# A 90-degree rotation of an 8192 x 8192 matrix: VectorE's grid copies move one output later in its order

## The chip, the cores and the metric

The kernel runs on one core of one Trainium2 chip. The metric is device time in microseconds (us) for one execution. The comparison value is the median of several runs.

## The reference

```python
def setup_inputs():
    return {"x": np.random.randn(8192, 8192).astype(np.float32), "k": 1}

def reference(x, k):
    return np.rot90(x, k)
```

With k = 1, output element (i, j) is x[j, 8191 - i]: a transpose and a reversal of the columns. Nothing is computed. 268.44 MB are read and 268.44 MB are written.

## The kernel before, in words

**Macros, tiles, outputs.** The matrix is cut into 16 macros (`macros`, line 54), numbered kk, each 1024 rows by 4096 columns. A macro arrives as T = 8 row tiles of 128 rows by 4096 columns (2 MB each) and leaves as J = 8 outputs (2 MB each). An output takes one chunk of 512 columns from all eight row tiles and is written as 512 rows by 1024 columns of the result. So 128 loads and 128 stores of 2 MB are made in all. Loads are numbered m = 8 kk + t and outputs n = 8 kk + j. In what follows, a dash marks the next macro: tile 0' is tile 0 of macro kk + 1.

**The grid.** A macro is held in a grid of 8 x 8 slots of 512 columns (`grid` in SBUF, line 61). Five corner slots are in PSUM (`corner`, line 62), and four of the grid places so freed serve as staging buffers for TensorE (`STAGES`, line 24). In an even macro a tile fills a row of slots and an output reads a column. In an odd macro it is the other way round. So the slots that output j has been read out of are just those that tile j of the next macro needs, and one grid holds two macros that interleave.

**Buffers.** There are five SBUF buffers of 2 MB. Loads use three at first and, after the ninth load, only two (`load_buf`, line 80). Outputs rotate over three (`out_buf`, line 83), except the last eight, which use all five.

**What each engine does.**

- SyncE (line 132) issues the loads. A load waits until the load that last used its buffer has been copied to the grid (`s_copy`, line 137).
- VectorE (line 146) does two things. `place(m)` (line 149) waits for the landing of tile m and copies its 4096 columns from the buffer to its grid slots, in one or two instructions (line 156). This frees the load buffer. `to_stage` (line 159) copies 512 columns per partition, reversed, to a staging buffer (line 166). A call waits until TensorE is done with the stage it reuses (line 163).
- TensorE (line 212) transposes each staged half block by four 128 x 128 matmuls with the identity into one of three PSUM banks (line 221).
- ScalarE (line 237) copies each bank to the output buffer (line 258), eight copies of 512 columns to an output, and then issues the store (line 265). Before an output's first copy it waits for the store that last used the buffer (line 244).

**VectorE's order.** It is written out by hand in lines 188 to 209, and it sets when the loads' buffers come free and when outputs start. An output with j > 0 is eight `to_stage` calls. Output 0 of a macro is made in `first(kk)` (line 173): eight `to_stage` calls, one for each tile. The first seven read from the grid. The eighth reads tile 7 straight from its load buffer after waiting for its landing, and tile 7 is placed right after. So the order in a macro is: output 0 and tile 7 (both in `first`), then tile 0', output 1, tile 1', output 2, tile 2', and so on to tile 6', output 7, and then `first` of the next macro. Put in loads: before output n is staged, VectorE has waited for the landing of load n + 7, at every n up to 120.

`first(0)` at the start works on tiles as they land. The last macro has no next one, so outputs 121 to 127 are staged without any load between them.

Of the kernel before, what the change touches and what calls it, by code (L numbers as in the profile page):

```python
# [10 lines left out]
T = R // P  # L11
W = 4096
G = 4
J = W // (G * P)
# [32 lines left out]
def kernel(tc: tile.TileContext, x: bass.AP, k: bass.AP, out: bass.AP):  # L47
# [10 lines left out]
    with tc.tile_critical():  # L58
# [15 lines left out]
        def stage(q):  # L74
            at = STAGES[q % len(STAGES)] * CH
            return grid[:, at : at + CH]
# [3 lines left out]
        def load_buf(m):  # L80
            return m % 3 if m <= T else (m + 1) % 2

        def out_buf(n):
            e = n - (n_out - J)
            if e < 0:
                return 2 + (n + 1) % 3
            free = [load_buf(n_load - 2), load_buf(n_load - 1)]
            free += [out_buf(n_out - J - 3 + i) for i in range(3)]
            return free[e % 5]
# [25 lines left out]
        with nc.Block() as block:  # L115

            @block.gpsimd
            def _(e):
                e.memset(ident[:], 0.0).then_inc(s_id, 1)  # L119
                e.wait_ge(s_id, 1)  # L120
                e.affine_select(  # L121
                    out=ident[:],
                    in_=ident[:],
                    compare_op=mybir.AluOpType.not_equal,
                    fill=1.0,
                    base=0,
                    pattern=[[-1, P]],
                    channel_multiplier=1,
                ).then_inc(s_id, 1)

            @block.sync
            def _(e):
                last = {}
                for m in range(n_load):
                    b = load_buf(m)
                    if b in last:
                        e.wait_ge(s_copy, last[b] + 1)
                    last[b] = m
                    r0, c0 = macros[m // T]
                    r0 += m % T * P  # L140
                    e.dma_start(
                        out=bufs[b][:], in_=x[r0 : r0 + P, c0 : c0 + W]
                    ).then_inc(s_land[b], 16)

            @block.vector
            def _(e):
                half = 0

                def place(m):
                    b = load_buf(m)  # L150
                    kk, t = divmod(m, T)
                    a = bufs[b][:].rearrange("p (j c) -> p j c", c=CH)
                    e.drain()
                    e.wait_ge(s_land[b], land_wait[m])
                    for at, n, v in pieces(*((0, t) if kk % 2 else (t, 0)), J, kk % 2):
                        i = e.tensor_copy(out=v, in_=a[:, at : at + n, :])  # L156
                    i.then_inc(s_copy, 1)

                def to_stage(srcs):

                    nonlocal half
                    if half >= len(STAGES):
                        e.wait_ge(s_pe, half - len(STAGES) + 1)
                    for at, v in srcs:
                        s = stage(half)[:, at * P : at * P + v.shape[1] * v.shape[2]]
                        i = e.tensor_copy(  # L166
                            out=s.rearrange("p (n c) -> p n c", n=v.shape[1]),
                            in_=v[:, :, ::-1],
                        )
                    i.then_inc(s_full, 1)  # L170
                    half += 1

                def first(kk):

                    for t in range(T):
                        m = kk * T + t
                        b = load_buf(m)
                        if kk == 0 or t == T - 1:
                            e.wait_ge(s_land[b], land_wait[m])
                            v = bufs[b][:, :CH].rearrange("p (n c) -> p n c", n=1)  # L180
                        else:
                            e.wait_ge(s_copy, m + 1)
                            ((_, _, v),) = pieces(*((0, t) if kk % 2 else (t, 0)), 1, False)
                        to_stage([(0, v)])
                        if kk == 0 or t == T - 1:
                            place(m)

                first(0)
                for n in range(n_out):
                    kk, j = divmod(n, J)  # L190
                    if j:
                        e.wait_ge(s_copy, T * (kk + 1))
                        for w in range(G):
                            for t in range(0, T, H):
                                to_stage(
                                    [
                                        (at, v[:, :, w * P : (w + 1) * P])
                                        for at, _, v in pieces(
                                            *((j, t) if kk % 2 else (t, j)),
                                            H,  # L200
                                            not kk % 2,
                                        )
                                    ]
                                )
                    if kk + 1 < len(macros):
                        if j < J - 1:
                            place(n + T)
                        else:
                            first(kk + 1)

            @block.tensor
            def _(e):
                halves = n_out * G * 2

                def run(n):
                    for q in range(n):
                        e.wait_ge(s_free, 1).then_inc(s_free, -1)
                        e.wait_ge(s_full, 1).then_inc(s_full, -1)  # L218
                        for t in range(H):
                            at = q % BANKS * CH + t * P  # L220
                            i = e.transpose(  # L221
                                ps[:, at : at + P],
                                stage(q)[:, t * P : (t + 1) * P],
                                ident[:],
                            )
                        i.then_inc(s_pe, 1)

                turns = e.alloc_register("turns")
                e.wait_ge(s_id, 2)
                e.reg_mov(turns, halves // LOOP)  # L230
                with e.While(lambda: e.snap(turns) > 0):
                    run(LOOP)
                    e.reg_sub(turns, turns, 1)
                run(halves % LOOP)

            @block.scalar
            def _(e):
                stored = [0] * 5
                e.sem_inc(s_free, BANKS)
                for n in range(n_out):  # L240
                    kk, j = divmod(n, J)
                    b = out_buf(n)
                    if stored[b]:
                        e.wait_ge(s_store[b], stored[b])
                    elif b < 3:
                        e.wait_ge(
                            s_copy, 1 + max(m for m in range(n_load) if load_buf(m) == b)
                        )
                    o = bufs[b][:].rearrange("p (g t c) -> p g t c", g=G, t=T)
                    for h in range(2 * G):  # L250
                        q = n * 2 * G + h
                        e.wait_ge(s_pe, q + 1)
                        src = ps[:, q % BANKS * CH : (q % BANKS + 1) * CH]
                        if j == 0:
                            dst = o[:, :, h, :]
                        else:
                            dst = o[:, G - 1 - h // 2, h % 2 * H : (h % 2 + 1) * H, :]
                        e.copy(  # L258
                            dst, src.rearrange("p (n c) -> p n c", n=H)
                        ).then_inc(s_free, 1)  # L260
                    e.drain().then_inc(s_act, 1)
                    e.wait_ge(s_act, n + 1)
                    r0, c0 = macros[kk]
                    top = M - c0 - (j + 1) * G * P
                    e.dma_start(
                        out=out[top : top + G * P, r0 : r0 + R].rearrange(
                            "(g m) f -> m g f", g=G
                        ),
                        in_=bufs[b][:].rearrange("m (g f) -> m g f", g=G),
                    ).then_inc(s_store[b], 16)  # L270
                    stored[b] += 16
                for b in range(5):
                    e.wait_ge(s_store[b], stored[b])
# [35 lines left out]
```

## Time and profile before

| What | Value |
|---|---|
| median of 3 runs | 1283.79 us (1281.51 to 1284.75) |
| the profiled execution's own time | 1281.77 us |
| its span, first to last instruction | 1280.0 us |
| moved by DMA | 537.09 MB, mean 420 GB/s over the span |
| TensorE matmul, busy | 723.3 us (57%) |
| VectorE, busy | 758.1 us (59%) |
| ScalarE, busy | 568.7 us (44%) |
| load, issue to landing, median | 17.2 us |
| store, issue to landing, median | 15.3 us |

How to read it: "busy" is the time in which an engine had an instruction at work. Of a DMA queue the profile gives the number of packets and the share of the 16 DMA engines' span that they took. q1 carries the loads that SyncE issues, q10 the stores that ScalarE issues, q14 the program's own instructions. A window line gives, for a stretch of the span, the busy time and the instruction count of each engine, the clock granted to TensorE, the DMA engines' mean busy share and the GB/s that they moved. A timeline line has start, length, engine, line of the code, operation, what it writes and reads, the count, and in brackets how long the engine was idle before and what ended that.

### The profile page before, as it was taken

What the parts mean: (1) busy time and instruction counts of PE and PEld (TensorE: products, weight loads), DVE (VectorE), ACT (ScalarE), POOL (GpSimd) and SP (SyncE); (2) the same over time, 40 slices, a digit from 0 to 9 for tenths busy, and PEclk for the clock granted to TensorE, in tenths of its full rate; (3) what the DMA queues carried; (4) which work ended last, traced back from release to release, by engine and by line L of the source; (5) the groups of instructions that cost most, each with busy time, mean ns of one, the idle gap of its engine ahead of it and who ended that gap; (6) DMA issues with size and microseconds to landing.
All of it is one profiled execution on the core that took longest, in us unless ns stands there. A gap on an engine that the chain in (4) does not pass through costs nothing. (4 is left out here: it accounts for less than half of the span.)

```text
span 1280.0 us, 13910 instructions
## 1 busy us (share of the span) xinstructions
PE 723.3 (57%) x4096; PEld 662.8 (52%) x4096; DVE 758.1 (59%) x1352; ACT 568.7 (44%) x1025; POOL 0.7 (0%) x6
## 2 busy tenths in 40 slices
PE   1456655556546556465564655655557465565666
PEld 1355654456546456454554545545446454554564
DVE  4657565565655656556565565655656556665574
ACT  1344544444444444344453444534445344453456
POOL 0000000000000000000000000000000000000000
PEclk9977767776877776877776777768776777786788
DMA  9999999999999999999999999999999999999979
GB/s 397 419 430 428 432 428 430 429 430 429 429 429 430 424 420 429 424 426 419 405 424 427 427 422 401 420 430 429 428 403 430 425 426 422 412 428 428 420 315 380
DMA packets 36889, 537.09 MB, mean 420 GB/s; under 512 B 4096, under 2 KB 4096, under 8 KB 4096
## 3 DMA queue, kind: packets, MB, share of 16 engines
q10 hardware_dynamic: 18432, 268.44, 49.9%
q1 hardware_dynamic: 18432, 268.44, 49.6%
q14 instruction: 25, 0.20, 0.0%
HBM read 268.44 MB, written 268.44 MB: 419 GB/s over the span
## 5 line engine op out<-in xcount | busy, mean ns | idle before, releaser
L221 PE MATMUL ps<-ident,grid 128*128 128x128 f32 x4096 | 723.3, 352 | 547.6 <-PEq L218 544.6
L221 PEld LDWEIGHTS ps<-ident,grid 128*128 128x128 f32 x4096 | 662.8, 188 | 607.9 <-issue 596.9
L258 ACT COPY buf<-ps 128x512 f32<-128x512 f32 x1024 | 567.4, 589 | 701.9 <-PE ps L221 698.4
L156 DVE COPY grid<-buf 128x4096 f32<-128x4096 f32 (+3 forms) x128 | 282.9, 2210 | 326.9 <-DMA buf<-in_x_dram 324.8
L166 DVE COPY grid<-grid 128x512 f32<-128x512 f32 (+2 forms) x1001 | 383.3, 409 | 148.3 <-PE ps L221 141.0
L166 DVE COPY grid<-corner 128x256 f32<-128x256 f32 (+2 forms) x160 | 66.8, 417 | 0.0
L156 DVE COPY corner<-buf 128x1024 f32<-128x1024 f32 (+2 forms) x40 | 48.8, 1220 | 0.0
L166 DVE COPY grid<-buf 128x512 f32<-128x512 f32 x23 | 9.8, 427 | 35.7 <-DMA buf<-in_x_dram 21.9
L258 ACT ACT_TABLE_LOAD x1 | 1.3, 1283 | 1.0 <-SPq L58 1.0
L121 POOL TENSOR_SCALAR_AFFINE_SELECT ident<-ident 128x128 f32<-128x128 f32 x1 | 0.3, 292 | 0.2 <-POOL ident L119 0.2
L119 POOL MEMSET ident<- 128x128 f32 x1 | 0.2, 204 | 0.5 <-SPq L58 0.5
L290 POOL MEMSET const-bfloat16-1.0<- 128x1 bf16 x1 | 0.1, 101 | 0.0
L290 POOL MEMSET const-uint8-127<- 128x1 uint8 x1 | 0.1, 101 | 0.0
L290 POOL MEMSET const-float32-0.0<- 128x1 f32 x1 | 0.1, 98 | 0.2 <-issue 0.2
L290 POOL MEMSET const-float32-1.0<- 128x1 f32 x1 | 0.1, 98 | 0.0
## 6 DMA issues: line engine op xcount, KB each, us to landing
buf<-in_x_dram SPq DMA_DIRECT2D x128, 2048.0 KB, 17.2
out_dram<-buf ACTq DMA_DIRECT2D x128, 2048.0 KB, 15.3
```

Source lines behind the costliest of these rows:

```text
L119: e.memset(ident[:], 0.0).then_inc(s_id, 1)
L121: e.affine_select(out=ident[:], in_=ident[:], compare_op=mybir.AluOpType.not_equal, fill=1.0, base=0, pattern=[[-1, P]], channel_multiplier=1,
L156: i = e.tensor_copy(out=v, in_=a[:, at : at + n, :])
L166: i = e.tensor_copy(out=s.rearrange("p (n c) -> p n c", n=v.shape[1]), in_=v[:, :, ::-1],)
L221: i = e.transpose(ps[:, at : at + P], stage(q)[:, t * P : (t + 1) * P], ident[:],)
L258: e.copy(dst, src.rearrange("p (n c) -> p n c", n=H)).then_inc(s_free, 1)
L290: nc = _bacc.Bacc("TRN2", target_bir_lowering=False, num_devices=1)
```

## The change

Only the place of `place` in VectorE's order changes. After output j the kernel copied tile j' (for j < 7). Now it copies tile (j - 1)' (for j > 0), and after output 7 it copies tile 6' and goes on to `first(kk + 1)`.

```diff
                     if kk + 1 < len(macros):
-                        if j < J - 1:
-                            place(n + T)
-                        else:
+                        if 0 < j:
+                            place(n - 1 + T)
+                        if j == J - 1:
                             first(kk + 1)
```

The order in a macro becomes: output 0 and tile 7 (in `first`), output 1, tile 0', output 2, tile 1', and so on to output 7, tile 6', and then `first` of the next macro. Output n with j > 0 is now staged after the landing of load n + 6, and output 0 of a macro still after that of load n + 7. The other engines' programs are the same instructions in the same order, with the same waits, and VectorE has the same instructions in another order.

## Prediction

> **What bounds the kernel now.** I read the page's slices and DMA queues first, then windows of the stretches, the list of waits, and VectorE's timeline at a macro's end and at the kernel's end.
>
> ```profile
> DMA  9999999999999999999999999999999999999979
> ...
> q10 hardware_dynamic: 18432, 268.44, 49.9%
> q1 hardware_dynamic: 18432, 268.44, 49.6%
> q14 instruction: 25, 0.20, 0.0%
> ```
> Loads (q1) and stores (q10) together fill the 16 DMA engines for 99.5% of the span. No compute engine is above 59%. The windows say where the rest is:
>
> ```profile
> 0.00:10.00 10.00, 1.09 (x4) 0.71 (x4) 1.59 (x2) 1.28 (x1) 0.70 (x6) 1.00 0.81 321
> 10.00:40.00 30.00, 6.52 (x24) 4.30 (x24) 17.33 (x15) 4.11 (x7) 0.00 (x0) 1.00 1.01 431
> ...
> 60.00:1220.00 1160.00, 666.01 (x3741) 615.30 (x3740) 689.23 (x1232) 519.71 (x936) 0.00 (x0) 0.75 1.01 424
> 1220.00:1280.00 60.00, 41.23 (x288) 34.66 (x286) 36.36 (x88) 38.37 (x72) 0.00 (x0) 0.87 0.82 344
> ```
> Of the last three columns the second is the DMA engines' busy share and the third the GB/s. From 10 us on, first with loads alone and then with both, the share is 1.0. Only the last 60 us fall to 0.82: some 11 us of DMA are lost there, and that is nearly all there is to win. The waits agree:
>
> ```profile
> DVE grid L156 <- DMA buf<-in_x_dram: 324.8, 105, 5.3
> DVE grid L166 <- PE ps L221: 154.8, 401, 0.9
> DVE grid L166 <- DMA buf<-in_x_dram: 21.9, 8, 8.3
> ```
> VectorE waits 324.8 us for landings, and no row shows ScalarE waiting for a store. So the middle is bound by DMA, whatever VectorE does, as long as both queues hold work. The end is another stage:
>
> ```profile
> 1206.39 2.29 DVE L156 COPY grid<-buf 128x4096 f32<-128x4096 f32 x1 [3.01 <-DMA buf<-in_x_dram]
> ...
> 1216.30 1.76 DVE L156 COPY grid<-buf 128x3072 f32<-128x3072 f32 x1 [3.15 <-DMA buf<-in_x_dram]
> 1217.97 1.22 DVE L156 COPY corner<-buf 128x1024 f32<-128x1024 f32 x1
> 1219.10 0.55 DVE L166 COPY grid<-grid 128x512 f32<-128x512 f32 x2
> ...
> 1229.33 0.43 DVE L166 COPY grid<-buf 128x512 f32<-128x512 f32 x1 [0.93 <-PE ps L221]
> 1229.85 2.82 DVE L156 COPY grid<-buf 128x2560 f32<-128x2560 f32 x1
> 1232.58 1.75 DVE L156 COPY corner<-buf 128x1536 f32<-128x1536 f32 x1
> 1234.37 2.11 DVE L166 COPY grid<-grid 128x512 f32<-128x512 f32 x6
> ```
> Loads 125 and 126 land at 1206.39 and 1216.30, so 9.9 us apart. The next and last, load 127, is due at 1226.2; the trace's semaphore marks say 1226.3. VectorE takes it up only at 1229.33, since it first stages output 119 (from 1219.10) and the seven grid chunks of output 120. After that there are no loads. Placing ends at 1234.33, and outputs 121 to 127 leave at ScalarE's pace: its store issues begin at 1241.11, 1246.06, 1251.00, 1256.33, 1261.28, 1266.22 and 1271.65, about 5.0 us apart (eight copies in 4.17 plus a gap of 0.77). The last store lands at 1278.3. So **the end is the last landing + 3.0 + 49.0 us**.
>
> **The change part by part.**
>
> *Work.* Nothing is added or removed: the same 1352 VectorE instructions, loads and stores. Every cost is one of order.
>
> *The shift.* Inside a macro the order stays copy, output, copy, output; only the output's number moves up. Output n follows landing n + 6, not n + 7, so its store is issued one landing, 9.9 us, earlier. As the DMA engines have no free time before 1220, a store served earlier is paid for by loads. With loads alone, tiles land 4.9 us apart (42.55 and 47.44 on VectorE's timeline); with stores beside them 9.9. One store before the last landing therefore puts that landing off by 4.9 to 5.0 us. Now, stores up to 118 are issued when load 127 lands (119 at 1227.05). Then, 119 will be issued right after landing 126 and, in the alternation of the two queues, stand about where 118 stands now. Bounds: 0 (the lead is lost again by then) to 5.0 (kept whole). I take **+4.9**, the upper end, since the share of 1.0 leaves no room to absorb it.
>
> *The end.* Output 119 is staged after landing 125 and over before landing 126. Tile 126 is placed at once (3.0 us), the seven chunks of output 120 take about 3 us, and VectorE then waits for landing 127. The 3.0 us between landing and copy go: **-3.0**. What is late next is the same chain of 49.0 us: 5.0 for the last chunk and placing tile 127, then ScalarE, whose 5.0 us for each output is hardly over a store's 4.9. DMA idles there as now, so stores that are already out don't shorten it. Bounds: -3.0 and 0.
>
> *The macro's end.* Here the pattern does change. At the macro's end near 590 us, landings come at 579.51 (tile 6'), 589.4 (7') and 598.63; store 7 is issued at 589.66, store 0' at 594.61, store 1' at 607.58. Afterwards store 7 goes out about 10.2 us after landing 5' (as 589.66 - 579.51), so 0.3 after landing 6'. Store 0' follows landing 7' by 0.1 + 2.7 (594.61 - 591.94), so at 2.8. The gap between these two stores grows from 5.0 to 12.4 us. A store lands 15.3 us after issue (median), so store 7 is in flight until 5.7 us after landing 7', past the issue of store 0'. And tile 7' is placed by 5.1 us after its landing, not 7.6 (596.95 - 589.4) as now, which lets SyncE issue the next load 2.5 us sooner. The cover is load 0'' (the next macro's first), in flight until about 9.9. I take 0. If the cover is gone, all engines idle from store 7's last byte to store 0'', at most a few us: bounds 0 and 2 us at each of 15 macro ends, 0 to 30 us. For a gain: the page's slices between 50 and 1220 us run from 401 to 432 GB/s; if a calmer order won 0.3 us at each macro end, -5 us.
>
> *The wait that moves.* Tile 0' of the next macro is now queued behind output 1's eight stagings, 4.7 us (600.84 to 605.3 by the same rows), and SyncE's load into its buffer behind that. VectorE is through at 5.1 + 4.7 = 9.8 us after landing 7'; tile 0' lands at 9.9. Cost 0; with the landing as early as 4.9 after, 5 us late, but another load is then in flight. Out buffers: a store's buffer is needed again three outputs, some 30 us, later, against 15.3.
>
> *The start.* Output 1 no longer waits for landing 8 (idle 1.48 us) and its copy (2.2): its store goes out some 3.7 us sooner. DMA is full there, so 0.
>
> *The sum.* +4.9 - 3.0 + 0 = **+1.9 us**. The profiled execution's 1281.77 (1280.0 of span) becomes 1283.7. That execution lies low among the runs (1281.51 to 1284.75); on the median of 1283.79 it gives 1285.7, and I say 1285.5, since the lead may be a tenth of a store short.
>
> One rule of the Trainium skill would make it worse. "DMA: Bandwidth & Descriptors", section "Bandwidth", says that for transfers between HBM and SBUF a limit of about 358 GB/s per core binds. The window of 10 to 40 us shows 431 and the whole span 420, so here the measurement decides. By the page one store of 2.10 MB would, as an estimate, cost the loads 5.9 us, and the sum would be +2.9.
>
> **The rivals.**
>
> *Store queue runs dry at each macro's end (slower).* For it: the gap of 12.4 us between stores 7 and 0', longer than the 9.9 in which the DMA engines move a load and a store, and a load buffer that is held until tile 7' is placed. An engine that is ahead of the slowest has then neither store nor load. Against: 15.3 us of a store's flight. It decides from 0.14 us per macro end on ((3.85 - 1.7)/15). At 0.4 us: +1.9 + 6, so 1291.7; at 0.7, 1296.2.
>
> *Loads are not put off (faster).* If the lead is gone at the last macro's end, because the gap before output 120 gives the loads the engines, the sum is -3.0: 1280.8. With the calmer macro ends, -3.0 - 5 = 1275.8. For it: 11 us of idle DMA at the end. Against: DMA share 1.0 up to 1220.
>
> *Nothing moves.* If outputs don't run ahead because ScalarE has no free buffer, VectorE hangs in the stage instead of at the landing and the time is 1283.8. Against: no such wait in the list, and 30 us against 15.3.
>
> **How the numbers follow.** About 0.3%, 3.85 us, is what a measurement of this kernel can tell from no change: 1279.9 to 1287.6 is "same". The forecast (1284 to 1287.5) has 0.45, dry queues 0.33 (1287.6 and up), loads not put off 0.16 (0.14 of it below 1279.9), nothing moves 0.06. Same: 0.45 + 0.02 + 0.06 = 0.53; slower 0.33; faster 0.14. The range of 1277 to 1294 leaves out the far part of the dry queues (0.13) and of the gain (0.05).
>
> **What the profile after will show.** Right, if load 127 lands near 1231, VectorE stages its chunk within 0.3 us, the last store is issued near 1273.5, and VectorE's waits for landings at line 166 (now 21.9 us, 8 times) appear at every macro's end. The shift is wrong if the last landing stays at 1226. The dry queue is shown by a DMA share under 0.97 in windows of 10 us around macro ends, and by a longer 60:1220 stretch. All of it is wrong if the GB/s of the middle, 424, moves by over 1%, which is 12 us.

## The result, and the profile after

The changed kernel takes 1277.85 us (median of 7 runs, 1276.63 to 1280.14) against 1282.03 us (7 runs, 1278.98 to 1286.32) for the kernel before. The ratio is 0.9964, with a 95% interval of [0.9947, 0.9982]. Measured again on another occasion it was 0.9984, [0.9975, 0.9994]. By these two ratios the kernel is 2 to 4.6 us faster, under half a per cent, and neither interval reaches 1. I had forecast 1.9 us slower.

The profiled execution took 1278.41 us, its span is 1276.6 us (before: 1281.77 and 1280.0). The windows of the changed kernel, with the same columns as before (the last three are TensorE's granted clock, DMA share and GB/s):

```profile
60.00:1220.00 1160.00, 670.83 (x3743) 619.07 (x3742) 685.30 (x1237) 520.93 (x936) 0.00 (x0) 0.76 1.01 426
1220.00:1280.00 60.00, 37.13 (x253) 31.03 (x251) 31.56 (x74) 34.41 (x64) 0.00 (x0) 0.82 0.74 313
```

The middle moved 426 GB/s instead of 424, at the same DMA share of 1.01. That is half a per cent, or some 5 us of 1160, but the loads are not 5 us ahead. By 1220 us the load packets add up to 268.33 MB in both profiles, and the store packets to 249.8 MB instead of 247.9. The difference is about one store of 2.1 MB. Next the DMA issues (median from issue to landing at the end of a row) and the waits (total us, times, longest):

```profile
buf<-in_x_dram SPq DMA_DIRECT2D x128, 2048.0 KB, 17.3
out_dram<-buf ACTq DMA_DIRECT2D x128, 2048.0 KB, 23.5
```

```profile
DVE grid L156 <- DMA buf<-in_x_dram: 299.2, 99, 5.4
DVE grid L166 <- PE ps L223: 136.0, 357, 0.9
ACT buf L260 <- DMA out_dram<-buf: 77.9, 24, 5.1
DVE grid L166 <- DMA buf<-in_x_dram: 70.5, 23, 8.3
```

A store now takes 23.5 us from issue to landing, not 15.3. So of the 9.9 us by which I had it issued earlier, 8.2 go into a longer time to landing. ScalarE, which never waited for a store, now waits 24 times for a free output buffer, 77.9 us in all. This wait varies from execution to execution. In the second measurement's profile (r_after below) it is 422.8 us in 93 waits. And VectorE waits for landings at line 166, as foretold, at each macro's end. VectorE's timeline at the end of the kernel:

```profile
1215.66 1.76 DVE L156 COPY grid<-buf 128x3072 f32<-128x3072 f32 x1 [2.56 <-DMA buf<-in_x_dram]
1217.34 1.22 DVE L156 COPY corner<-buf 128x1024 f32<-128x1024 f32 x1
1218.47 1.42 DVE L166 COPY grid<-grid 128x512 f32<-128x512 f32 x4
...
1225.43 0.43 DVE L166 COPY grid<-buf 128x512 f32<-128x512 f32 x1 [3.08 <-DMA buf<-in_x_dram]
1225.95 2.82 DVE L156 COPY grid<-buf 128x2560 f32<-128x2560 f32 x1
1228.69 1.75 DVE L156 COPY corner<-buf 128x1536 f32<-128x1536 f32 x1
1230.47 1.43 DVE L166 COPY grid<-grid 128x512 f32<-128x512 f32 x4
```

Load 126 lands at 1215.66, load 127 at 1225.4, and the row at 1225.43 shows VectorE waiting for it. Before it came 3.0 us late. The last store lands at 1275.0, which is 49.6 us after the last landing (before: 52.1). The last landing itself is not at 1231, where I had it, but at 1225.4, 0.9 us earlier than before.

### The profile page after: what moved, and what is told of

It is laid out like the page before. It is cut to its first block, busy times and chain, and to the rows that moved or that the text cites. A ratio compares the mean times of both kernels' runs of the same rounds, so it can differ in the third digit from the quotient of the medians.

```text
span 1276.6 us, 13910 instructions
## 1 busy us (share of the span) xinstructions
PE 727.7 (57%) x4096; PEld 665.7 (52%) x4096; DVE 752.2 (59%) x1352; ACT 570.0 (45%) x1025; POOL 0.7 (0%) x6
## 5 line engine op out<-in xcount | busy, mean ns | idle before, releaser
L166 DVE COPY grid<-grid 128x512 f32<-128x512 f32 (+2 forms) x1001 | 377.1, 409 | 141.1 <-PE ps L223 136.0
L156 DVE COPY corner<-buf 128x1024 f32<-128x1024 f32 (+2 forms) x40 | 48.8, 1220 | 0.0
## 6 DMA issues: line engine op xcount, KB each, us to landing
out_dram<-buf ACTq DMA_DIRECT2D x128, 2048.0 KB, 23.5
```

The lines of the kernel that those rows point to most:

```text
L166: i = e.tensor_copy(out=s.rearrange("p (n c) -> p n c", n=v.shape[1]), in_=v[:, :, ::-1],)
```

## The experiments

All are small edits of the written-out order at the end of VectorE's loop, or transfers alone. The edits of the order are shown against the changed kernel, those of the transfers against the kernel before, and all are shortened. Each ratio is against the kernel before as run on the same occasion, with its 95% interval. "Last landing" is the landing mark of load 127 in the kernel's profile, "end part" the time from it to the last store's landing. "Slow" is worked out from the packet records. (These name no engine. Packets that follow each other without a gap I take for one engine's.) A 16 KB packet takes 0.61 us; for those over 0.7 us I add up what is above 0.61 and divide by 16 engines. Profile columns are of one execution each, and executions of one kernel differ by 2 to 9 us, so the ratio decides. The profile of f5 is that of its slowest execution of 12 (1284.89 us, median 1281.08).

| Kernel | Ratio to before | Last landing | End part | Slow, us |
|---|---|---|---|---|
| before | | 1226.3 | 52.1 | 15.4 |
| changed | 0.9964 [0.9947, 0.9982] | 1225.4 | 49.6 | 11.1 |
| changed, r_after | 0.9984 [0.9975, 0.9994] | 1228.1 | 48.9 | 13.8 |
| e1_last_only | 0.9971 [0.9958, 0.9985] | 1226.9 | 50.0 | 14.7 |
| e2_all_but_last | 0.9988 [0.9978, 0.9998] | 1224.5 | 52.1 | 11.1 |
| e3_tile6_only | 0.9955 [0.9938, 0.9971] | 1222.9 | 49.5 | 12.1 |
| e4_middle_only | 1.0001 [0.9992, 1.0011] | 1226.8 | 52.8 | 13.1 |
| f4_tile6_last | 0.9984 [0.9972, 0.9996] | 1228.2 | 49.4 | 15.9 |
| f5_old_start | 0.9997 [0.9985, 1.0009] | 1232.1 | 49.4 | 14.3 |
| g1_two_ahead | 1.0029 [1.0015, 1.0043] | 1232.4 | 50.3 | 16.4 |
| h0_first_only | 0.9998 [0.9983, 1.0012] | 1227.6 | 51.6 | 16.2 |
| h3_tile6_not_last | 0.9965 [0.9951, 0.9979] | 1222.9 | 51.8 | 11.7 |

After the result I held to the step of my forecast that a store ahead is paid for by loads (theory A), and put the gain down to faster packets in the middle. The rival B was that the gain is all at the end.

**e1_last_only**: the new order in macro 14 only.

```diff
-if 0 < j:
+if kk < len(macros) - 2:
+    if j < J - 1:
+        place(n + T)
+elif 0 < j:
     place(n - 1 + T)
```

> VectorE's new order only in macro 14, the one before the last; the old order in all others. Theory A (the changed kernel wins in the middle: a store that starts on a store queue which still holds packets moves at full rate, one that starts on a drained queue makes packets slow; the lead of one store at the end costs the loads some 4.2 us and takes VectorE's 3.0 us of lateness away): no gain in the middle, so +4.2 - 3.0 = about +1 us beside the kernel before, last landing near 1230. Rival B (the gain is all at the end: VectorE is free at the last landing and loads aren't put off at all; the middle differs by chance): -3 to -4 us, as the whole change, with the last landing where it was.

Measured: 0.9971, -3.7 us, with the last landing at 1226.9, 0.7 later than before. Store 118 is issued at 1206.4, not at 1215.3, and yet theory A's +4.2 on the last landing is not there. Quicker packets don't hide it either: slow packets cost 14.7 us here and 15.4 before. The gain of the end can be had with one macro's order.

**e2_all_but_last**: the reverse, the old order in macro 14 only (`kk == len(macros) - 2` in the same edit).

> The new order in macros 0 to 13, the old one in macro 14. Theory A: the middle wins what it wins in the changed kernel, the lead is given back before the end and VectorE is late by 3.0 us again: about -4.4 us beside the kernel before (a little better than the changed kernel's), last landing near 1222. Rival B: 0 us, within 1.5.

Measured: 0.9988, -1.5 us. The end part is back at 52.1. The middle is worth something, less than A wanted, about what B allowed for chance.

**e3_tile6_only**: only tile 6 of each macro is moved behind output 7.

```diff
-if 0 < j:
-    place(n - 1 + T)
+if j < J - 2:
+    place(n + T)
 if j == J - 1:
+    place(n - 1 + T)
     first(kk + 1)
```

> The old order, but tile 6 of the next macro is placed after output 7 instead of before it, in every macro; the other tiles as before. So only the last output of each macro runs ahead. Theory A: the store queue is fuller only around each macro's end, so part of the gain, 0 to -2 us in the middle, and at the end +4.2 - 3.0: in sum -1 to +1 us. Rival B: VectorE is free at the last landing, so -3 to -4 us.

Measured: 0.9955, -5.8 us, more than either theory expected, and no less than the whole change, whose interval overlaps. Its last landing is at 1222.9. The end of the kernel on VectorE's timeline:

```profile
1218.95 2.60 DVE L166 COPY grid<-grid 128x512 f32<-128x512 f32 x7
1222.95 0.43 DVE L166 COPY grid<-buf 128x512 f32<-128x512 f32 x1 [1.41 <-DMA buf<-in_x_dram]
```

VectorE is in time, as in the changed kernel.

**e4_middle_only**: outputs 1 to 6 run ahead, tile 6 is placed before output 7 as of old.

```diff
-if 0 < j:
+if 0 < j < J - 1:
     place(n - 1 + T)
+if j == J - 2:
+    place(n + T)
```

> The new order for outputs 1 to 6 of each macro, but tile 6 is placed before output 7, as in the kernel before, so that the macro's end is the old one. Theory A: outputs 1 to 6 run ahead and keep the store queue filled, the end as before: -3 to -4 us beside the kernel before. Rival B: VectorE is late by 3.0 us at the last landing as before, so 0 us, within 1.5.

Measured: 1.0001, so theory A's -3 to -4 is not there either: outputs that run ahead of landings win nothing in this form. It is not a clean test of them, though. To give the lead back, VectorE places tiles 5' and 6' with no output between, and in the profile loads land 4.9 to 17.8 us apart (8.0 to 12.2 before).

So I asked directly what a store issued ahead costs. Three kernels have no compute: loads as in the kernel with two buffers, each issued when the load two before has landed, and stores of a constant with one, two or three in flight, one execution each. Theory C is that the DMA engines take load and store packets in turns, so that a store issued ahead only waits longer in its own queue.

```diff
+DEPTH = 2    # 1, 2, 3
...
+if n >= DEPTH:
+    e.wait_ge(s_store[n % DEPTH], 16 * (n // DEPTH))
 e.dma_start(out=..., in_=...).then_inc(s_store[n % DEPTH], 16)
```

**d1_dma_only**

> Loads and stores alone, with no compute: 128 loads of 2 MB with two buffers (each issued when the load two before has landed), and 128 stores of a constant, of which one is in flight at a time; the output is that constant. The store queue runs dry between two stores. Theory A (each store issued ahead takes its whole 4.9 us from the loads): loads are far ahead of the stores, the store rate is what one in flight gives. Theory C (the engines take load and store packets in turns; a store issued ahead only waits in its own queue): the same here, loads take the engines in the gaps, landings under 9 us apart. Only the slow packets are at issue: if a start on a dry store queue makes packets slow, over 0.15 us lost per store, 15 us or more in all; if not, under 5 us.

Measured: 2.1 us of slow packets, 50 of the 68 in the first 100 us. Loads land 7.4 us apart on average (5.5 to 9.1 for the middle eight tenths), and the last at 935.0 us. Every store after the first starts on an empty store queue, 127 in all, but only 63 of them while loads still run, not the 119 that a later expectation names. An empty queue beside running loads doesn't by itself make packets slow.

**d2_dma_only** and **d3_dma_only**

> As the run with one store in flight, but two in flight, so that the store queue always holds packets. Landings of loads about 9.8 us apart, last load landing near 1240. Slow packets: under 3 us in all if a filled queue prevents them.

> As the run with two stores in flight, but three, so one more store is issued ahead at any time. Theory A: that store is served at the loads' cost, so the last load lands 4 to 5 us later than with two in flight. Theory C: it waits in its queue, the store's time from issue to landing grows from about 20 to about 29 us, and the last load lands within 1 us of the run with two in flight.

The DMA issues with two stores in flight, and then with three:

```profile
buf<-in_x_dram SPq DMA_DIRECT2D x128, 2048.0 KB, 19.5
out_dram<-buf ACTq DMA_DIRECT2D x128, 2048.0 KB, 19.5
```

```profile
buf<-in_x_dram SPq DMA_DIRECT2D x128, 2048.0 KB, 19.5
out_dram<-buf ACTq DMA_DIRECT2D x128, 2048.0 KB, 29.2
```

With one more store issued ahead all the time, stores wait 9.7 us longer, loads take 19.5 us as before, and the last load lands at 1210.3 us in both. The cost of a store ahead, which I had put at 4.9 us, is 0. Theory C holds where the store queue isn't empty. The Trainium skill says the same of the engines: "DMA: Bandwidth & Descriptors", section "Queues, rings and completion order", has each DMA engine go round the queues that hold work, a packet at a time, and loads and stores of 19.5 us each in d2 agree with it. (Both kernels' last loads landed earlier than the 1240 that I had expected.)

Where the store queue does run empty, a store ahead isn't free. With one store in flight (d1) a store goes out about every 14 us while loads run, and loads land 7.4 us apart. With two (d2) both come every 9.8 us, and the last load lands at 1210.3 us instead of 935.0.

**f4_tile6_last**: tile 6 moved in macro 14 alone, one tile in the whole kernel.

```diff
-if 0 < j:
-    place(n - 1 + T)
+if kk < len(macros) - 2 and j < J - 1 or j < J - 2:
+    place(n + T)
+elif kk == len(macros) - 2 and j == J - 1:
+    place(n - 1 + T)
```

> The old order everywhere, but in macro 14 tile 6 of the last macro is placed after output 7 instead of before it: one copy moved in the whole kernel. Theory C (the two queues alternate packet by packet, so a store issued ahead doesn't put loads off; the gain is VectorE's lateness of 3.0 us at the last landing, and a small rest in the middle): -3 us beside the kernel before, the last landing not later. Theory A (a store issued ahead is paid for by the loads): +1 us. If the gain of the kernel with tile 6 moved in every macro (-5.4 us) comes from one place, this kernel shows the same -5.4.

Measured: 0.9984, -2.0 us, and an end part of 49.4. This is the price of VectorE's lateness by itself, with an interval of -0.5 to -3.6 us. It is not the whole -5.8 of e3.

**f5_old_start**: the new order, but macro 0 keeps the old one.

```diff
-if 0 < j:
+if kk == 0:
+    if j < J - 1:
+        place(n + T)
+elif 0 < j:
     place(n - 1 + T)
```

> The new order in all macros but the first, which keeps the old one. At the start the store queue is empty, so this is where a store sent earlier does get the engines: the changed kernel has 0.3 of a store more behind it than the kernel before from there on. Theory C: without it the loads win back 0.3 x 4.9 = 1.5 us, so about -5.5 us beside the kernel before, against -4.2 for the changed kernel. Theory A: no difference from the changed kernel within 1 us.

Measured: 0.9997. A miss for both: its end part is short (49.4), so its middle must be some 2 us worse than that of the kernel before. Nothing here explains that.

**g1_two_ahead**: two outputs ahead from macro 1 on.

```diff
-if 0 < j:
+if kk == 0 and 0 < j:
     place(n - 1 + T)
+elif 1 < j:
+    place(n - 2 + T)
 if j == J - 1:
+    if kk:
+        place(n - 1 + T)
     first(kk + 1)
```

> From the second macro on tiles are placed two outputs later than in the kernel before (after output j tile j - 2, and tiles 5 and 6 after output 7), so outputs run two ahead; the first macro as in the changed kernel. Theory A: another store ahead, 4 to 5 us slower than the changed kernel. Theory C: stores wait longer in their queue (issue to landing near 30 us), ScalarE waits more for free output buffers, landings stay 9.9 us apart: as the changed kernel within 2 us, unless VectorE, held up behind ScalarE, places tiles so late that the load queue runs dry.

Measured: 1.0029, +3.7 us. Its waits:

```profile
DVE grid L166 <- PE ps L227: 178.6, 301, 4.6
ACT buf L264 <- DMA out_dram<-buf: 162.9, 39, 6.4
```

ScalarE waits 162.9 us for output buffers, and VectorE's longest wait for TensorE is 4.6 us (0.9 before). That fits the turn to slower at the end of C's expectation: VectorE, held up in the stage, places tiles late. It doesn't show it, because the changed kernel in r_after has longer waits for buffers (422.8 us), a longest wait for TensorE of 3.2 us, and is faster than the kernel before. Nor is theory A ruled out by this run alone. It wanted 4 to 5 us more than the changed kernel, and 5.7 to 8.3 were measured. What makes g1 slow stays open.

**r_after**, **h0_first_only**, **h3_tile6_not_last**: the changed kernel again; the new order in macro 0 only (`if kk:` old, else new); and e3's edit without macro 14 (`kk == len(macros) - 2` keeps the old order).

> The changed kernel itself, on the same chip as the two others of this call, so that their middles can be set beside it. -4 us (-3 to -6) beside the kernel before.

> The new order in macro 0 only, the old one in all others: the complement of the kernel that keeps the old order in macro 0. Theory D (the middle's rest comes from the order at each macro's end, not from the start): 0 us beside the kernel before, within 1.5. Theory E (the first macro's order sets the phase of stores against loads for the whole run, and the slow packets with it): -2 to -4 us, with the last landing some 3 us earlier and VectorE still 3 us late at it.

> Tile 6 placed after output 7 in macros 0 to 13, the old order in macro 14: the complement of the kernel with this one copy moved in macro 14 alone (-2.0 us), and together with it the kernel with the copy moved everywhere (-5.8). Theory D: -3 to -4 us, all in the middle, VectorE still 3 us late at the last landing. If the middle's gain there was chance: 0 us, within 1.5.

Measured: 0.9984, 0.9998 and 0.9965. The start carries nothing, so theory E falls. The macro ends carry -4.5 us with VectorE still late at the last landing (end part 51.8). h3 and f4 are the two parts of e3, and -4.5 and -2.0 make -6.5 against its -5.8. Windows of the kernel before, of h3 and of f4:

```profile
60.00:400.00 340.00, 200.26 (x1115) 186.06 (x1113) 201.29 (x360) 154.55 (x279) 0.00 (x0) 0.74 1.01 429
400.00:800.00 400.00, 227.40 (x1283) 209.51 (x1281) 238.25 (x421) 178.62 (x322) 0.00 (x0) 0.76 1.01 421
800.00:1200.00 400.00, 226.83 (x1284) 208.96 (x1285) 238.09 (x430) 177.62 (x320) 0.00 (x0) 0.75 1.01 424
```

```profile
60.00:400.00 340.00, 190.18 (x1115) 173.01 (x1113) 200.56 (x361) 153.75 (x280) 0.00 (x0) 0.76 1.01 429
400.00:800.00 400.00, 224.82 (x1285) 205.64 (x1286) 238.41 (x426) 177.01 (x320) 0.00 (x0) 0.75 1.01 425
800.00:1200.00 400.00, 227.74 (x1298) 208.24 (x1297) 236.60 (x429) 178.83 (x324) 0.00 (x0) 0.74 1.01 423
```

```profile
60.00:400.00 340.00, 191.59 (x1108) 174.54 (x1108) 200.71 (x360) 153.16 (x279) 0.00 (x0) 0.77 1.01 427
400.00:800.00 400.00, 228.75 (x1280) 211.42 (x1280) 236.26 (x420) 176.98 (x320) 0.00 (x0) 0.75 1.01 420
800.00:1200.00 400.00, 225.94 (x1280) 207.92 (x1280) 237.51 (x426) 177.25 (x322) 0.00 (x0) 0.76 1.00 424
```

The DMA share is 1.0 everywhere, and still the GB/s differ: 421 and 420 between 400 and 800 us with the old macro ends, 425 with tile 6 moved (the changed kernel: 426). One per cent of 400 us is 4 us, which is the size of h3's gain. The slow packets agree. As the mark of their start I take the first 100 us after 60 with over 20 of them. In the four profiles with the old order in macros 1 to 13 it begins at 300 us (e1, f4) or 400 (before, h0). In the six with tile 6 behind output 7 at those macro ends and outputs at most one ahead it begins at 500 (e3, h3), 600 (changed, e2, f5) or 700 (r_after). So in these profiles, one of each kernel, the order at the macro's end goes with later slow packets. That this makes the whole gain isn't shown: f5 has the late start too and gains nothing.

**d1_with_copies** and **d2_with_copies**: the transfers alone, with one and with two stores in flight, and VectorE copying blocks next to them.

```diff
+for i in range(560):
+    e.drain()
+    e.tensor_copy(out=grid[:, i % 7 * F : (i % 7 + 1) * F], in_=bufs[3 + i % 2][:])
```

> The transfers-only kernel with one store in flight, and VectorE copying 128 x 4096 blocks all the time from the buffers that the stores read; the output is a constant. The transfers alone lost 2.1 us to slow packets with 119 starts on a dry store queue, so a dry queue alone isn't the cause. If it is a dry queue together with a compute engine at work in SBUF, over 10 us of slow packets; if the cause is neither, under 5.

> The same with two stores in flight, so that the store queue never runs dry. If slow packets need a dry queue and a compute engine at work, under 3 us, as without copies (1.6); if VectorE's copies alone make them, 10 us or more.

Measured: 6.8 us of slow packets with one store in flight (2.1 without copies) and 2.0 with two (1.6 without). Copies beside an emptying queue go with more slow packets, copies beside a filled one don't. But 6.8 us lies between the two marks that I had set, 5 and 10, and under the 15.4 of the kernel before. Nor are the two alike: here only 62 stores start on an empty queue while loads run. So whether copies and an emptying queue are the whole cause stays open. (The whole-kernel time of these two is set by the copies or by the single store, and says nothing.)

## Why the prediction was wrong, step by step

- **What bounds the kernel**: right for the middle. DMA share is 1.0 between 60 and 1220 us in every kernel with compute, and transfers alone with two stores in flight take 1257.5 us as a whole. But it is an average. In the last 10 us before the last landing the kernel before already had room (see the shift).
- **The end, -3.0**: right in kind, and about right in size. The end part shrinks from 52.1 to 49.6, and in all kernels that free VectorE at the last landing it is 48.9 to 50.3, in all that don't 51.6 to 52.8. f4, which does nothing else, gives -2.0 us.
- **The shift, +4.9**: this is the step that failed. I wrote that a store served earlier is paid for by loads, and that the share of 1.0 leaves no room. But load 127 landed at 1225.4 and, in r_after, at 1228.1, against 1226.3 before. In e1, where only macro 14 changes, it landed 0.7 us later. In d2 against d3 the cost of a store issued ahead is 0. The reason is that a landing is that of the slowest of 16 engines. On the engine that lands last, a store that is issued earlier is hardly served earlier: between 1219.7 and 1225.8 the packets of load 127 and of stores alternate there one by one. Store 118 lands 1.4 us after load 127 instead of 2.6, because two of its packets instead of four are left on that engine. So two more packets of 0.61 us were through by then, 1.2 us and not 4.9. On the other engines the earlier store is served earlier. When store 118 is issued in the kernel before, 12 of the 16 have nothing left of the store ahead of it, and half of them are done with store 118 itself by 1223.9 us; after the change by 1216.5. But half the engines finish load 127 by 1219.1 us before and by 1218.9 after, 6 us ahead of the last, so what they serve early costs nothing. The same small price shows at the start, where the lead is built up. Load 15 lands 1.5 to 1.7 us later than before in the six profiles with outputs ahead in macro 0, and between 0.3 earlier and 0.7 later in the five others. The room was to be seen before the change, in a window that ends with the last landing (DMA share 0.81):

```profile
1216.00:1226.00 10.00, 6.34 (x32) 6.37 (x33) 7.83 (x17) 3.65 (x7) 0.00 (x0) 0.66 0.81 333
```

- **The macro's end, 0**: wrong as well, by the size that I had kept as the bound of a gain. I named a possible cause (tile 7' is placed 2.5 us sooner and the next load issued sooner) and took 0. h3 measures -4.5 us for moving tile 6 behind output 7, 0.3 us at each of 14 macro ends. In e2, which has this and outputs that run ahead, -1.5 are left. Whether the sooner load is the cause no run here shows.
- **Outputs ahead, out buffers**: "30 us, later, against 15.3" failed with the shift: at 23.5 us, ScalarE waits 77.9 us for buffers, at 24.2 in r_after 422.8. In e4 running ahead wins nothing, in g1 more of it loses. The changed kernel, -2 to -4.6, is no better than e3, -5.8, which moves tile 6 alone.
- **The rivals**: "loads are not put off" is what happened, with its price of -3.0 and some of the -5 of the macro ends. I gave it 0.16, with the lead lost at the last gap as the reason. The lead isn't lost, it is served where it costs no landing. So its number came close for another reason. Dry queues at macro ends didn't come: the lowest share in any window of 10 us between 60 and 1220 is 0.98, as before (0.96, once, in r_after).
- **The sum**: the profiled executions' spans differ by -3.4 us. Of that -2.5 is the end part and -0.9 the last landing. The latter splits into +1.2 for the shift and about -2.0 of time on the engine that lands last which its start and its packets at 0.61 us don't account for (19.0 us up to load 127 before, 17.0 after). This -2.0 is a remainder, so that the sum comes out proves nothing. That it is faster packets is not shown.
- **A small slip**: the output's eight stagings behind tile 7' take 4.4 us by the rows that I named (600.84 to 605.28), not 4.7. After the change they took 4.7 (594.06 to 598.74), and the term stayed 0.

What stays open: why packets are slower at some times. In the kernels with compute they set in somewhere between 200 and 700 us and then mostly keep on; the transfers alone show 50 of 68, 50 of 52 and 42 of 44 (d1, d2, d3) in the first 100 us. An emptying store queue (d1) isn't enough, VectorE's copies beside a filled queue (d2_with_copies) aren't, and both together give 6.8 us with half as many starts. How the order at the macro's end wins its 4.5 us, why f5 wins nothing and why g1 loses is open as well.

## What to carry to other kernels

When two DMA queues share saturated engines, ask which of them is empty at the moment, on the engine that lands last. In d2 and d3 a store issued earlier into a queue that already held work only waited there, at no cost to the loads and at no gain. From d1 to d2, where it filled an empty queue, the loads paid for it. The gain is then where an engine stands between a landing and what follows it. Here one moved tile at the last macro, and the same at each macro's end, did no less than the whole change: e3_tile6_only has 0.9955.

## What the runs showed of the hardware

- A busy share of 1.0 doesn't mean full speed. Packets of 16 KB take 0.61 us, and in the kernel before 655 of 32768 took over 0.7 us, some near 1.9. The 400 us from 400 on moved at 421 GB/s instead of the 430 of the transfers alone, with the same share of 1.01.
- The DMA engines don't stay together. In the kernel before, 12 of the 16 ended the last load by 1219.4 us and one at 1225.8, and the landing at 1226.3 follows the slowest.
- An engine with packets of both queues takes them in turns. On the one that landed last, load and store packets alternated between 1219.7 and 1225.8 us, each 0.61 us long.
- Loads and stores together moved 430 GB/s with two stores in flight, as much as loads alone did (431 between 10 and 40 us).
